# Probabilities copied by pairs of tiles, and a head in another order, in a two-group hybrid attention layer

## The chip, the cores and the metric

The kernel runs on one core of one Trainium2 chip. The metric is the device time of one execution in microseconds (us); lower is better. The times before are those of three runs.

## The reference, cut to what matters

One encoder layer is applied to two groups of 1024 rows (`prompt` and `sample`, called group 0 and group 1 here) with the same weights; the model width is 1024.

```python
mod = silu(c) @ w_ada + b_ada
shift, scale, gate = split(mod, 3)
h = rms_norm(x, norm_g) * (1 + scale) + shift
qa, ka, va, za, qb, kb, vb, zb, ga, gb = split(h @ w_in)
# branch A: 8 query heads, 2 key heads of 64; RMS norm of q and k, axial rotary positions
oa = gqa_attention(qa, ka, va) * silu(za)
# branch B: 4 heads, two softmax maps each, p0 - lam * p1, values of 128
ob = diff_attention(qb, kb, vb, lam)
ob = rms_norm(ob, subln_g) * (1 - lam_init) * silu(zb)
merged = sigmoid(ga) * (oa @ w_proj_a) + sigmoid(gb) * (ob @ w_proj_b)
y = x + gate * (merged @ w_out)
```

Softmax runs over all 1024 keys. Everything is float32; the large projections are done as three products of operands split into a high and a low part.

## The kernel before, in words

**Staging.** Python generators issue small pieces of work, and `weave` interleaves them by a planned count and a lead for each stream (`Z_SHARE`, `ATT_W`, `IN_A` and the other constants at the top are those counts and leads). A scheduler of the language then puts each engine's instructions in order by priority and gives tiles their slots; engines called through `act`, `vec`, `pe` and `dma_next` keep the program's order. All transfers are issued by one queue, SP, in its order.

The stages of a group: the modulation and h (`start`, `start_late` for group 0, `ht_gen` for group 1); the *head* (`head`: keys and values of A, the first queries of A); attention A in 32 units, interleaved with projections (`qa_gen`, `qkb_gen`, `vb_gen`) and with gate-path projections ("z work": `z_gen`, L881, used as filler); attention B in 16 units, of which the last four are interleaved with the rest of the z work and the first merges (`fill`, `gates`, `merge_gen`); then merge and output projection (L1170, L1201) alone.

**Attention.** A *tile* is the softmax of 128 queries over 1024 keys: four matmuls of 512 columns into a two-bank PSUM tile (L908, L909), a maximum on VectorE (L910), an exponential on ScalarE into an SBUF tile p (L912), and in `flip` a 32x32 block transpose on VectorE (L953) and four copies issued by SP (L958) that put the four 32-partition strips where the product with v wants them, in a tile `pT` that holds two tiles (t = 0 and 1). In A a unit is two heads' tiles and the product with v is L984; in B a unit is four tiles (two query tiles, two maps each), the second map is first subtracted (L939, L940, L952), and the product is L1021. The p tiles are 5 buffers of 1024 columns. They also hold the staged first weights (`load_quarters`), the early rows of the head (`row_early`), group 1's x (`ht_gen`) and the sigmoid gates read back in `merge_gen`.

**Group 0's head.** While h of the first 512 rows is made by quarters, `sums_early` already adds up the key/value and first query products of row tiles 0 to 3 (the "early rows"). Then, in `head`: two steps of z, the norm of the late 512 rows (`late[0]`), two steps of z, eight steps of z woven with the late rows' h (`late[1]`), then the early rows' norm and rotary work (`rows`, `rope`, half of it on GpSimd), then the later row tiles woven with z. Each row tile's end, `pairs_T` (L730 to L733), transposes it on TensorE and splits it on ScalarE and VectorE.

**The residual's gate.** `gate_gen` reads the last third of `w_ada` (4 MB) in two halves into weight tiles `wg`, and makes the gate from 32 matmuls of 256 columns (L602) and eight small ones (L611). It is an item of the z work, after the seventh item, and so runs in attention A of group 0.

**The first z weights.** `start` loads them (`load_w`, L244) after the late rows' x (`load_xT0(1)`), splits them on ScalarE (L208) and VectorE (L209), and z begins with them.

Of the kernel before, what the change touches and what calls it, by code (L numbers as in the profile page):

```python
# [20 lines left out]
P = 128  # L21
# [16 lines left out]
    (6, 21, 4, 2, 4, 4),  # L38
    (13, 12, 5, 3, 2, 6),
)  # L40
Z_HEAD = (7, 6)
Z_HEAD_A = (-0.216, -0.32)
ATT_W = (
    (0.893, 1.067, 1.068, 1.192, 1.03, 1.769),
    (1.237, 1.862, 1.041, 1.418, 0.645, 1.256),
)
IN_A = (
    (0.205, -0.07, 0.861, 0.05, 0.25, 0.15),
    (0.125, -0.05, 0.368, 0.3, -0.03, 0.694),
)  # L50
Z_A = (
    (0.2, 0.05, 0.62, -0.05, -0.1, -0.05),
    (-0.215, 0.07, 0.2, 0.16, -0.3, -0.1),
)
LAST_ATT = (46, 40)
LAST_FILL = (20, 25)
GATED_A = (0.063, -0.144)
LATE_A = 1.197
QUARTER_P = 202
KV_STEPS = 12  # L60
GATE_AT = 6
FIRST_ATT = 12
FIRST_A = 0.26
TAIL = (3, 3)
TAIL_A = (0.92, 1.2)
LAG = 2
Z_FIRST = (12, 6)
Z_FIRST_A = (0.017, -0.452)
# [44 lines left out]
def kernel(ctx: ExitStack, tc: tile.TileContext, t: dict):  # L113
# [7 lines left out]
    ppool = ent(tc.tile_pool(name="ppool", bufs=5))  # L121
# [42 lines left out]

    def ptile():
        return ppool.tile([P, 1024], F32, tag="p", name=nm("p"))
# [4 lines left out]
    def halves(pt):  # L171
        return pt[:, :1024], pt[:, 1024:]

# [45 lines left out]
    def load_quarters(mat, col):  # L219
# [3 lines left out]
        sts = [x.rearrange("p (c n) -> p c n", c=2) for _ in range(2) for x in halves2(ptile())]  # L223
# [7 lines left out]
    def load_w(pieces, room=None):  # L231

        if room is None:
# [5 lines left out]
        for q in range(4):  # L239
# [7 lines left out]
            split_w(w, q, st)  # L247
        return [w[c // 2][:, c % 2] for c in range(NCH)]
# [191 lines left out]
    def start(ht):  # L440
# [63 lines left out]
        kva_w.append((load_w(w_cols(w_in, (z_col(Z_ORDER[0]), 256)), room=(utile(), utile())),))  # L504
        sq = late_squares(xT[1])
        return lambda: inv_rms(sq, pe), lambda rs: start_late(ht, xT[1], rs)
# [80 lines left out]
    def gate_gen():  # L587
        for half in range(2):
            w = wpool.tile([P, NCH, 512], F32, tag="w", name=nm("wg"))
            for q in range(4):  # L590
                row, col = q * 256, 2 * D + half * 512
                dma(
                    w[:, q * 2 : q * 2 + 2],
                    w_ada[row : row + 256, col : col + 512].rearrange("(c p) n -> p c n", p=P),
                )
            for n in (half * 2, half * 2 + 1):
                cols = slice(n % 2 * 256, n % 2 * 256 + 256)
                acc = gbank()[:, :256]
                nc.vector.memset(acc, 0.0)
                for q in range(2):  # L600
                    for c in range(4):
                        nc.tensor.matmul(  # L602
                            acc[32 * c : 32 * c + 2], cT[:, q * 4 + c], w[:, q * 4 + c, cols], start=(q == 0),
                            stop=(q == 1), tile_position=(0, 32 * c),
                        )
                    yield 1
                part = rtile()[:, :256]
                nc.vector.tensor_copy(part, acc)
                ps = gbank()[:, :4].rearrange("p (c g) -> p c g", g=2)
                for c in range(2):  # L610
                    nc.tensor.matmul(ps[:, c, :], part[:, c * P : (c + 1) * P], two, start=True, stop=True)  # L611
                cs = slice(n * 2, n * 2 + 2)
                nc.vector.tensor_tensor(
                    out=gatec[:, cs], in0=ps, in1=bcol[:, 2, cs].unsqueeze(2).to_broadcast([P, 2, 2]), op=ALU.add
                )
                nc.vector.tensor_scalar(out=gatec[:, cs], in0=gatec[:, cs], scalar1=0.5, scalar2=None, op0=ALU.mult)
# [812 lines left out]
```

## Time and profile before

| what | value |
|---|---|
| median of three runs | 1884.54 us (1883.9 to 1887.2) |
| the profiled execution's own time | 1887.84 us |
| its span | 1885.6 us |
| TensorE busy | 1852.3 us, 98% of the span |
| VectorE / ScalarE / GpSimd busy | 65% / 45% / 19% |
| copies of p to pT | 768, of 128 KB |

The profile is of one execution. PE is TensorE, PEld its weight loads, DVE VectorE, ACT ScalarE, POOL GpSimd, SPq the queue that issues transfers. In a timeline row the first two columns are start and length in us, then engine, line, operation, output<-input, shape, a count where like instructions follow each other, and in brackets the idle time before them and what ended it. A busy TensorE is not one at its peak: its clock can be halved, which the column PEclk of a windows view shows.

### The profile page before, as it was taken

What the parts mean: (1) busy time and instruction counts of PE and PEld (TensorE: products, weight loads), DVE (VectorE), ACT (ScalarE), POOL (GpSimd) and SP (SyncE); (2) the same over time, 40 slices, a digit from 0 to 9 for tenths busy, and PEclk for the clock granted to TensorE, in tenths of its full rate; (3) what the DMA queues carried; (4) which work ended last, traced back from release to release, by engine and by line L of the source; (5) the groups of instructions that cost most, each with busy time, mean ns of one, the idle gap of its engine ahead of it and who ended that gap; (6) DMA issues with size and microseconds to landing.
All of it is one profiled execution on the core that took longest, in us unless ns stands there. A gap on an engine that the chain in (4) does not pass through costs nothing.

```text
span 1885.6 us, 32132 instructions
## 1 busy us (share of the span) xinstructions
PE 1852.3 (98%) x11516; PEld 1599.4 (85%) x11516; DVE 1228.1 (65%) x1904; ACT 843.1 (45%) x1801; POOL 364.2 (19%) x692
## 2 busy tenths in 40 slices
PE   9999999999999999999999999999999999999999
PEld 7888888877889998788889888888888989877887
DVE  4756776465478677877464777666547767786731
ACT  3544554443456555524223555444445545552210
POOL 0342200011335152100134210000233513210000
PEclk9999999999999999999999999999999999999999
DMA  9225676676254536887531467776524344579532
GB/s 333 83 72 138 162 201 180 173 215 166 71 134 105 130 91 182 254 286 236 190 122 51 127 180 197 196 181 179 158 78 121 98 107 115 156 230 302 168 106 78
DMA packets 277612, 299.54 MB, mean 159 GB/s; under 512 B 37648, under 2 KB 228304, under 8 KB 277456
## 3 DMA queue, kind: packets, MB, share of 16 engines
q1 hardware_dynamic: 277456, 297.51, 55.6%
q8 instruction: 92, 1.51, 0.3%
q14 instruction: 64, 0.52, 0.1%
HBM read 137.91 MB, written 42.04 MB: 95 GB/s over the span
## 4 chain that ended last, share of the span: by engine, by line
PE 76%; DMA 7%; DVE 7%; SPq 3%; issue 3%; POOL 2%; ACT 2%; DVEq 0%; ACTq 0%; POOLq 0%
PE f L881 21%; PE f L670 18%; PE f L1201 6%; PE a L984 6%; PE f L1170 5%; PE s L908 5%; PE s L909 5%; PE a L1021 4%; PE s L1201 3%; DMA row<-zd 2%; PE s L1170 2%; DVE m L910 2%; SPq L958 1%; SPq L109 1%; DMA st<-in_w_in_dram 1%
## 5 line engine op out<-in xcount | busy, mean ns | idle before, releaser
L881 PE MATMUL f<-u,w 128*128 128x512 f32 x2088 | 524.9, 394 | 0.3 <-DVE u L733 0.3
L670 PE MATMUL f<-w,u 128*128 128x256 f32 x3264 | 448.2, 285 | 0.3 <-ACT ev L863 0.3
L881 PEld LDWEIGHTS f<-u,w 128*128 128x128 f32 x2088 | 382.7, 188 | 76.0 <-PE f L730 0.7
L670 PEld LDWEIGHTS f<-w,u 128*128 128x128 f32 x3264 | 425.2, 191 | 18.4 <-issue 1.4
L910 DVE TENSOR_REDUCE m<-s 128x1 f32<-128x1024 f32 x256 | 309.7, 1218 | 112.6 <-PE s L909 110.6
L953 DVE STREAM_TRANSPOSE p<-p 128x1024 f32<-128x1024 f32 x192 | 238.5, 1242 | 45.8 <-ACT p L912 42.1
L909 PE MATMUL s<-u,sw 128*128 128x512 f32 x512 | 202.9, 398 | 0.0
L209 DVE TENSOR_TENSOR w<-st,w 128x512 fp32r<-128x512 f32 x184 | 123.3, 699 | 82.4 <-ACT w L208 81.8
L208 ACT ACTIVATE w<-st 128x512 fp32r<-128x512 f32 x184 | 107.6, 626 | 133.5 <-DMA st<-in_w_in_dram 60.6
L912 ACT ACTIVATE p<-s,m,rsA 128x1024 f32<-128x1024 f32 x128 | 154.4, 1206 | 5.7 <-DMA q<-p 2.2
L912 ACT ACTIVATE p<-s,m,rsB 128x1024 f32<-128x1024 f32 x128 | 154.4, 1206 | 4.0 <-DMA q<-p 0.5
L695 POOL TENSOR_TENSOR rsB<-ss,nhalf 128x4 f32<-128x4 f32 x64 | 66.4, 1038 | 457.0 <-DVE ss L694 442.7
L1170 PE MATMUL f<-u,w 128*128 128x512 f32 x588 | 142.4, 391 | 0.2 <-DVE u L1181 0.2
L1021 PE MATMUL a<-q,u 128*128 128x256 f32 x512 | 126.1, 388 | 7.5 <-DMA q<-p 4.1
L1170 PEld LDWEIGHTS f<-u,w 128*128 128x128 f32 x588 | 109.9, 188 | 23.6 <-DVE u L1181 0.6
L984 PE MATMUL a<-q,u 128*64 128x128 f32 x2048 | 121.8, 276 | 4.0 <-DMA q<-p 3.9
L984 PEld LDWEIGHTS a<-q,u 128*64 128x64 f32 x2048 | 113.2, 138 | 14.6 <-issue 13.3
L733 DVE TENSOR_TENSOR u<-f,u 64x256 fp32r<-64x256 f32 (+1 forms) x208 | 83.7, 407 | 62.8 <-ACT u L732 57.5
L1021 PEld LDWEIGHTS a<-q,u 128*128 128x128 f32 x512 | 96.6, 194 | 23.0 <-issue 5.3
L1201 PE MATMUL f<-u,w 128*128 128x512 f32 x480 | 111.2, 389 | 0.0
L909 PEld LDWEIGHTS s<-u,sw 128*128 128x128 f32 x512 | 96.6, 189 | 16.2
L908 PE MATMUL s<-u 128*128 128x512 f32 x256 | 107.2, 421 | 2.6 <-ACT p L912 2.5
(208 smaller groups left out, 2152.1 us busy)
## 6 DMA issues: line engine op xcount, KB each, us to landing
q<-p SPq DMA_DIRECT2D x768, 128.0 KB, 2.8
st<-in_w_in_dram SPq DMA_DIRECT2D x128, 256.0 KB, 3.2
zd<-ev SPq DMA_DIRECT2D x96, 256.0 KB, 2.3
sw<-u SPq DMA_DIRECT2D x256, 64.0 KB, 2.1
p<-zd SPq DMA_DIRECT2D x64, 256.0 KB, 5.1
u<-in_w_ada_dram SPq DMA_DIRECT2D x16, 512.0 KB, 8.8
od<-oo SPq DMA_DIRECT2D x64, 128.0 KB, 2.6
st<-in_w_in_dram SPq DMA_DIRECT2D x64, 128.0 KB, 2.9
```

What stands on the lines that cost most here:

```text
L209: nc.vector.tensor_tensor(out=wl, in0=st, in1=wh.bitcast(F32), op=ALU.subtract)
L670: nc.tensor.matmul(ps, lt[c][:, sl], w[c][:, wi, :], start=(k == 0), stop=(k == 23))
L881: nc.tensor.matmul(ps, w[c][:, wi, e * P : (e + 1) * P], rt[c], start=(k == 0), stop=(k == 23),)
L908: nc.tensor.matmul(s[:, sl], q, k[:, sl], start=True, stop=False)
L909: nc.tensor.matmul(s[:, sl], sw, k[:, sl], start=False, stop=True)
L910: nc.vector.tensor_reduce(out=m, in_=s, axis=AX.X, op=ALU.max, negate=True)
L912: nc.scalar.activation(pt.rearrange("p (j c a) -> p j c a", j=4, c=8), s.rearrange("p (c a j) -> p j c a", c=8, j=4), AF.Exp, scale=rs, bi ...
L953: nc.vector.transpose(pt, pt)
L984: nc.tensor.matmul(acc[e * 64 : e * 64 + 64, n * P : n * P + P], u["v"](k), blocks[n][:, e, k], start=(k == 0 and n == 1), stop=(k == 7 an ...
L1021: nc.tensor.matmul(acc, u["v"][:, k], pT[:, k], start=(k == 0), stop=(k == 7))
L1170: nc.tensor.matmul(ps, w[:, c, wi, d * P : (d + 1) * P], o[:, oi, :], start=(k == 0), stop=(k == 11))
L1201: nc.tensor.matmul(ps, w[c][:, wi, e * P : (e + 1) * P], m[:, mi, :], start=(k == 0), stop=(k == 23))
```

## The change

- p tiles become two buffers of 2048 columns that hold a pair (t = 0 and 1), and one buffer of 1024 columns (`p1pool`) for the second map in B. The exponential writes its tile in four blocks of 256 columns, 512 apart, so that one copy per 32-partition strip moves both tiles: four issues of 256 KB per pair, after the second transpose, in place of four of 128 KB after each.
- `gate_gen` moves into group 0's head: weights in two halves of 2 MB into tiles of `upool`, issued in program order, the matmuls in the way of `ada_half` (8 of 512 columns for each half), the copy on ScalarE. The `wg` tiles go.
- The early rows' norm and rotary work becomes a stream `early_rows` of eight steps, woven with the late rows' h, the eight z steps and the gate's first half; the gate's second half is woven with the later row tiles.
- The first z weights: three of four quarters are issued ahead of the late rows' x.
- `merge_gen` reads four gates at a time, for the first branch into a tile of `upool` and for the second into a pair tile.
- The counts and leads are others: z steps in group 0 after the first twelve are 14+6 in the head (12+6 before), then 3 x (4, 17, 5, 1, 6) by phase (3 x (6, 21, 4, 2, 4) before, where 8 steps were the gate's).

```diff
-    (6, 21, 4, 2, 4, 4),
+    (4, 17, 5, 1, 6, 4),
...
-LAST_ATT = (46, 40)
-LAST_FILL = (20, 25)
+LAST_ATT = (47, 41)
+LAST_FILL = (23, 28)
...
-LATE_A = 1.197
+LATE_A = 1.334
+EARLY_A = 0.939
...
-GATE_AT = 6
+GATE_A = (0.074, -0.836)
...
-Z_FIRST = (12, 6)
-Z_FIRST_A = (0.017, -0.452)
+Z_FIRST = (14, 6)
+Z_FIRST_A = (-0.245, -0.338)
...
-    ppool = ent(tc.tile_pool(name="ppool", bufs=5))
+    ppool = ent(tc.tile_pool(name="ppool", bufs=2))
+    p1pool = ent(tc.tile_pool(name="p1pool", bufs=1))
...
+    def p2tile():
+        return ppool.tile([P, 2048], F32, tag="p", name=nm("p"))
     def ptile():
-        return ppool.tile([P, 1024], F32, tag="p", name=nm("p"))
+        return p1pool.tile([P, 1024], F32, tag="p1", name=nm("p1"))
...
-        for q in range(4):
+        def load(q):
             st = spool.tile([P, 2, 256], F32, tag="st", name=nm("st"))
...
+        if room:
+            for q in range(3):
+                load(q)
+            yield
+        for q in range(4):
+            if q == len(sts):
+                load(q)
+            split_w(w, q, sts[q])
...
             q_load(q)
+        z_first = load_w_steps(w_cols(w_in, (z_col(Z_ORDER[0]), 256)), room=(utile(), utile()))
+        next(z_first)
         xT.append(load_xT0(1))
...
+    def gate_gen(cpad):
         for half in range(2):
...
+                wt = chunks4(utile().bitcast(F32))
+                wts.append(wt)
+                for c in (0, 2):
+                    row = q * 512 + c * P
+                    dma_next(wt[:, c : c + 2], w_ada[row : row + 256, col : col + 512].rearrange("(c p) n -> p c n", p=P))
+            yield 1
+            acc = ada_half(wts[1], cpad, 1, ada_half(wts[0], cpad, 0))
+            yield 1
+            part = rtile()
+            nc.scalar.activation(part, acc, AF.Copy)
+            yield 1
+            ps = gbank()[:, :8].rearrange("p (c g) -> p c g", g=2)
+            for c in range(4):
+                nc.tensor.matmul(ps[:, c], part[:, c * P : (c + 1) * P], two, start=True, stop=True)
...
-            pt.rearrange("p (j c a) -> p j c a", j=4, c=8), s.rearrange("p (c a j) -> p j c a", c=8, j=4),
+            pt.rearrange("p j (c a) -> p j c a", c=8), s.rearrange("p (c a j) -> p j c a", c=8, j=4),
...
-        pt = ptile()
+        if i == 0:
+            u["p"] = p2tile()
+        both = u["p"].rearrange("p (j t f) -> p t j f", j=4, t=2)
...
+        pt = ptile().rearrange("p (j f) -> p j f", j=4) if m else both[:, t]
...
         nc.vector.transpose(pt, pt)
-        if t == 0:
+        if t:
             u["pT"] = pair(F32R)
-        dst = u["pT"].bitcast(F32).rearrange("p (i t f) -> p i t f", i=4, t=2)
-        for i in range(4):
-            dma(dst[:, i, t], pt[i * 32 : i * 32 + 32])
+            for i in range(4):
+                dma(u["pT"].bitcast(F32)[:, i * 512 : i * 512 + 512], u["p"][i * 32 : i * 32 + 32])
...
+                    if d == 0:
+                        gg = chunks4(p2tile() if br else utile().bitcast(F32))
+                        for a in range(4):
+                            dma(gg[:, a, :], st["gbd" if br else "gad"][(dt_ + a, hf)])
...
+        def early_rows(*gens):
+            for gen in gens:
+                for _ in range(4):
+                    held[0] = True
+                    drain(islice(gen, 3))
+                    held[0] = False
+                    yield 1
...
+            gate = late[2]
+            next(gate)
             drain(islice(zs, 2))
-            weave((islice(zs, 12 - 2 - 2), 12 - 2 - 2, 0.0), (late[1](rs), 4, LATE_A))
-            held[0] = True
-            drain(islice(kva, 12), islice(qa, 12))
-            held[0] = False
-            weave((kva, 15, 0.0), (islice(zs, Z_FIRST[0]), Z_FIRST[0], Z_FIRST_A[0]))
+            weave((islice(zs, 12 - 2 - 2), 12 - 2 - 2, 0.0), (late[1](rs), 4, LATE_A), (early_rows(kva, qa), 8, EARLY_A), (islice(gate, 3), 3, GATE_A[0]))
+            next(gate)
+            weave((kva, 15, 0.0), (islice(zs, Z_FIRST[0]), Z_FIRST[0], Z_FIRST_A[0]), (islice(gate, 3), 3, GATE_A[1]))
             next(qa)
...
-            items.insert(GATE_AT + 1, gate_gen())
```

More of the change, by code (lines that the diff above doesn't have):

```diff
@@ L172, in halves, with fours @@
         return pt[:, :1024], pt[:, 1024:]
+    def fours(pt):
+        return [pt[:, i * 512 : i * 512 + 512] for i in range(4)]
     def halves2(pt):
@@ L222, in load_quarters @@
         w = [w[:, q * 2 : q * 2 + 2] for q in range(4)]
-        sts = [x.rearrange("p (c n) -> p c n", c=2) for _ in range(2) for x in halves2(ptile())]
+        sts = [x.rearrange("p (c n) -> p c n", c=2) for x in fours(p2tile())]
         def load(q):
@@ L231, in load_w, with drain_last, load_w_steps @@
     def load_w(pieces, room=None):
+        return drain_last(load_w_steps(pieces, room))
+    def drain_last(steps):
+        for w in steps:
+            pass
+        return w
+    def load_w_steps(pieces, room=None):
         if room is None:
@@ L246, in load_w @@
             assert off == 256
-            split_w(w, q, st)
-        return [w[c // 2][:, c % 2] for c in range(NCH)]
+            sts.append(st)
+        if room:
[6 more added lines that the diff above has]
+            split_w(w, q, sts[q])
+        yield [w[c // 2][:, c % 2] for c in range(NCH)]
     def w_cols(mat, *cols):
@@ L584, in load_tables_A @@
             st[name] = tab
-    def gate_gen():
+    def gate_gen(cpad):
         for half in range(2):
[L589 to L616, printed above, removed]
@@ new lines, in gate_gen @@
+            col = 2 * D + half * 512
+            wts = []
+            for q in range(2):
+                wt = chunks4(utile().bitcast(F32))
[7 more added lines that the diff above has]
+            part = rtile()
@@ L620, in ht_gen @@
         for tt in range(NTT):
-            xt = ptile()
+            if tt % 2 == 0:
+                xts = halves(p2tile())
+            xt = xts[tt % 2]
             dma(xt, x_sample[tt * P : (tt + 1) * P])
@@ L639, in ht_gen @@
         for c in range(NCH):
-            xt = ptile()
+            if c % 2 == 0:
+                xts = halves(p2tile())
+            xt = xts[c % 2]
             dma(xt, xT_in[g][c * P : (c + 1) * P])
@@ L681, in row_early @@
         if not spare:
[L682 removed]
+            spare.extend(fours(p2tile()))
         return spare.pop(0)
```

38 lines of the change are left out of this document (21 added, 17 removed).

## The prediction

> **What bounds the kernel now.** I read the page's first two parts, then TensorE's waits, then its timeline wherever it stood idle, and last, for each of these places, the queue or engine that came late.
>
> ```profile
> span 1885.6 us, 32132 instructions
> PE 1852.3 (98%) x11516; PEld 1599.4 (85%) x11516; DVE 1228.1 (65%) x1904; ACT 843.1 (45%) x1801; POOL 364.2 (19%) x692
> ```
>
> TensorE is the bound: of the span it stands idle 1885.6 - 1852.3 = 33.3 us. Nothing that shortens another engine's work counts unless one of these idle stretches hangs on it. What ends them:
>
> ```profile
> PE a L1021 <- DMA q<-p: 4.1, 3, 2.7
> PE a L984 <- DMA q<-p: 3.9, 2, 2.3
> PE s L908 <- ACT p L912: 3.8, 4, 1.6
> PE a L1021 <- DVE r L939: 2.9, 1, 2.9
> PE f L602 <- DMA wg<-in_w_ada_dram: 1.4, 3, 0.7
> ```
>
> Columns are the total, the number of times and the longest. The copies of p end 8.0 us of idle time, but five times only, out of 64 products with v. The places, in order of time:
>
> ```profile
> 48.33 1.05 PE L109 MATMUL f<-two,row 128*128 128x2 f32 x8 [1.73 <-ACT row L109]
> 50.76 5.86 PE L881 MATMUL f<-u,u 128*128 128x512 f32 x18
> 64.41 5.73 PE L881 MATMUL f<-u,u 128*128 128x512 f32 x24
> 90.84 0.43 PE L730 MATMUL f<-ident,p 128*128 128x128 f32 x2 [0.89 <-POOL p L784]
> 119.69 0.33 PE L730 MATMUL f<-ident,row 128*128 128x128 f32 x1 [2.34 <-DVE u L733]
> 266.37 0.50 PE L908 MATMUL s<-u,u 128*128 128x512 f32 x1 [0.83 <-ACT p L912]
> 299.98 5.38 PE L984 MATMUL a<-q,u 128*64 128x128 f32 x64 [2.35 <-DMA q<-p]
> 420.62 3.91 PE L984 MATMUL a<-q,u 128*64 128x128 f32 x64 [1.51 <-DMA q<-p]
> 781.12 5.38 PE L1021 MATMUL a<-q,u 128*128 128x256 f32 x16 [2.65 <-DMA q<-p]
> 823.28 3.69 PE L1021 MATMUL a<-q,u 128*128 128x256 f32 x16 [0.77 <-DMA q<-p]
> 1692.19 0.50 PE L908 MATMUL s<-u 128*128 128x512 f32 x1 [1.63 <-ACT p L912]
> 1701.81 5.38 PE L1021 MATMUL a<-q,u 128*128 128x256 f32 x16 [2.88 <-DVE r L939]
> ```
>
> A stall costs more than its idle time. The same 16 matmuls of L1021 took 5.38 us after 2.65 us idle and 3.69 us after 0.77: 1.69 more. The windows view shows why:
>
> ```profile
> 51.00:54.60 3.60, 3.60 (x10) 2.79 (x10) 3.36 (x8) 3.60 (x8) 0.00 (x0) 0.56 0.51 153
> 122.80:126.30 3.50, 3.50 (x19) 3.40 (x19) 1.64 (x4) 1.12 (x3) 0.00 (x0) 0.56 0.51 100
> 300.00:305.40 5.40, 5.40 (x65) 5.23 (x66) 0.35 (x1) 0.56 (x2) 0.00 (x0) 0.69 0.72 209
> 1075.00:1400.00 325.00, 325.00 (x2454) 282.27 (x2453) 203.84 (x263) 155.03 (x325) 33.66 (x63) 1.00 0.63 166
> ```
>
> The third number from the end is the granted clock: 0.56 and 0.69 in the few us behind the stalls of 1.73, 2.34 and 2.35 us, which is 3.2 to 3.4 us at half speed (3.6 x 0.44 / 0.5 and 5.4 x 0.31 / 0.5). So a stall of some 2 us costs its length plus 1.7. The last row is group 1's attention A, with the same copies: TensorE busy 325 of 325 us. There the pairs can win nothing; all of the gain has to come from the places above.
>
> **The change part by part.** The sum is made against the profiled execution's 1887.84 us (its span and 2.2 us around it), 3.3 above the median of the runs.
>
> *First z weights ahead of the late rows' x: -3.5.* ScalarE runs in order:
>
> ```profile
> 47.16 0.63 ACT L208 ACTIVATE u<-st 128x512 fp32r<-128x512 f32 x1 [6.86 <-DMA st<-in_w_in_dram]
> 47.70 0.58 ACT L109 ACTIVATE row<-f 128x512 f32<-128x512 f32 x1
> 37.99 9.15 DMA st<-in_w_in_dram
> ```
>
> The copy `row`, which ends the modulation's last quarter, stands behind the split of z's first weights, and these, issued at 37.99 behind 2 MB of x, land at 47.14. TensorE waits 1.73 us for `row`, and the 18 matmuls behind ran at half clock: 5.86 us, where 24 later took 5.73, that is 18 x 0.239 = 4.3 (1.6 more, 1.7 by the clock). With the weights ahead of x the wait has no cause. What is late next: x, by the 768 KB moved ahead of it; it is read by ScalarE's squares after the last quarter, with the z matmuls of the early rows as cover. Ends: -1.7 (the clock window falls elsewhere) and -3.5.
>
> *The gate moved: -3.7.*
>
> ```profile
> L602 PE MATMUL f<-wg,cT 128*2 128x256 f32 x64 | 6.0, 378 | 1.4 <-DMA wg<-in_w_ada_dram 1.4
> 43.06 1.92 PE L109 MATMUL f<-u,at 128*32 128x512 f32 x16
> ```
>
> The 32 matmuls of 256 columns (64 records) cost 6.0 us. The second row is 8 matmuls of 512 columns by `ada_half` (16 records); the gate now takes 16 of them, twice that: 3.8. That is -2.2; the eight small sums stay. The 1.4 us of waiting for `wg` goes, with most of what the eight 512 KB loads do to SP and to weight tiles there: -1.5. In the head the two halves are filler: each half's loads are four issues more on SP, behind the z weights of the second item and ahead of nothing that TensorE waits for in the trace. ScalarE gets two copies and VectorE loses some, all under z matmuls. If that cover is gone, TensorE waits for 2 MB at the head's start. Ends: -5 and 0.
>
> *Early rows beside the late rows' h: -3.5.* Now their rotary work starts late on GpSimd and TensorE runs out of z at its end:
>
> ```profile
> 80.22 0.70 POOL L695 TENSOR_TENSOR rs<-ss,nhalf 128x2 f32<-128x2 f32 x1 [13.72 <-ACT u L109]
> 119.05 0.59 POOL L719 TENSOR_TENSOR row<-rc,row 128x128 f32<-128x128 f32 x1
> 86.50 0.74 DVE L109 SCALAR_TENSOR_TENSOR u<-u,modc,u 128x512 fp32r<-128x512 f32 x1
> ```
>
> GpSimd is idle 13.7 us before it begins on them; the last key tile is rotated at 119.64, and TensorE, at the end of its 12 z steps, waits 2.34 for it and 1.7 more by the clock; another 0.89 at 90.84. Starting 10 us earlier and two more z steps (each 8 matmuls of 0.239: 1.9) cover 3.8 us, more than the 2.34. That would be -0.9 - 2.3 - 1.7 = -4.9. Against it, VectorE makes the last piece of late h at 87.2, which the later row tiles need, and the early rows' share of VectorE now lies beside it. Ends: -4.9 and +6 (a rival below). I take -3.5, nearer the first, because the scheduler already put part of these rows ahead of 86.50.
>
> *Half the copies, in attention A of group 0: -5.*
>
> ```profile
> L958 SPq DMA_DIRECT2D q<-p x768: 542/602/1864, 135.3 to 1721.7; - x192
> L953 DVE STREAM_TRANSPOSE p<-p x192: 1217/1245/1248, 134.0 to 1716.1; 128x1024 f32<-128x1024 f32 x192
> 286.56 2.58 SPq L958 DMA_DIRECT2D q<-p  x4
> 289.83 7.68 SPq L958 DMA_DIRECT2D q<-p  x12
> q<-p SPq DMA_DIRECT2D x768, 128.0 KB, 2.8
> sw<-u SPq DMA_DIRECT2D x256, 64.0 KB, 2.1
> ```
>
> An issue takes SP 602 ns. I take the same for one of twice the bytes, since the number of rows written (128) stays, so 384 fewer are 231 us of SP; were it twice as long, SP would win nothing. The stall at 299.98 is SP's: it had fallen behind, issued sixteen copies of four tiles to 297.5, and the product waited for the last to land. As pairs, eight issues, it is through 4.8 us sooner, more than the 2.35. So 2.35 + 1.7 go; of the 0.83 at 266.37 and the 1.51 at 420.62 (both behind the same queue) I count half: 1.2. Sum -5.2, taken as -5. Cost: the copies are 256 KB. From 64 to 128 KB the landing grew 0.7 us (2.1 to 2.8), so another 128 KB costs between 0 and 1.4; I take 0.7, the middle. Tile t = 0 can no longer go ahead, but the products use both tiles. Behind the waiting SP stand only loads for later items.
>
> Two pair buffers in place of five tiles: a unit's first exponential now waits for the pair two units before. Group 1's 32 units of A lie about in the 325 us window above, some 10 us apart; transpose, four issues and landing after a unit's last exponential are 1.25 + 2.4 + 3.5 = 7.2, so under 3 us are left, and I count nothing. If that cover is gone, each us of it stops ScalarE once a unit. Writing in four blocks costs nothing while ScalarE (45%) and VectorE (65%) hide it; 10% on a transpose would be 0.12 us a tile.
>
> *The last units of B: -2.* Both groups: 2.65 + 0.77 there are copies, 1.63 and 2.88 are VectorE's and ScalarE's order, 1.7 twice the clock: 11.3 in all. The queue is lighter, the four gates no longer take p tiles, and group 0 keeps two more z steps for it (144 steps less 12, 20 and 99 leave 13; 152 with the gate's less 12, 18 and 111 left 11), 3.8 us of cover. But the landing is later and VectorE's order is drawn anew. Ends -11 and +25 (the third rival); I take -2, near nothing, because the copies that a product waited for were the last of its pair before as well.
>
> *New stalls: +3.* Another order brings its own. I charge one of the size of the smallest above, 0.8, with a clock window, rounded up.
>
> Sum: -3.5 - 3.7 - 3.5 - 5 - 2 + 3 = -14.7. 1887.84 - 14.7 = 1873.1; less the 3.3 of the profiled execution, 1870.
>
> **The rivals.**
>
> *The copies were hidden anyway.* Group 1's attention A has no stall with all 768 issues in place, which speaks for it; the sixteen issues at 286.56 speak against. Then only the first z weights and the matmuls of the gate stay, and new stalls take 3: -3.5 - 2.2 + 3 = -2.7, or 1882.
>
> *The head gets slower.* VectorE and GpSimd hinder each other:
>
> ```profile
> 66.53 0.29 DVE L784 TENSOR_TENSOR p<-p,rs 128x128 f32<-128x128 f32 x1
> 94.74 0.54 DVE L784 TENSOR_TENSOR row<-row,rs 128x128 f32<-128x128 f32 x1 [1.93 <-POOL rs L695]
> 94.67 0.46 POOL L709 TENSOR_TENSOR rc<-p,tab 128x128 f32<-128x128 f32 x1
> ```
>
> The same VectorE product took 0.29 alone and 0.54 beside GpSimd. Late h is 16 operations of 0.74; if a dozen lose 0.25 each that is 3 us, and 3 us of the early rows' own VectorE work slips ahead: late h ends 6 us later, with TensorE waiting. Then +6 stands for -3.5: 1870 + 9.5 = 1879.5. The Trainium skill, SBUF — State Buffer, section "SBUF: two separate sides", says the two engines take a shared pair of ports as an exclusive lock, so that the loser blocks for the whole instruction; by that rule this rival would be the full price. The 0.54 agrees with it.
>
> *Landing decides, slower than before.* The last four units of B in each group have the least z to cover a late pT. If the copies of all eight units land 1.4 us later than now, with a clock window for each, that is 8 x 3.1 = 25; with the first z weights, the gate and attention A kept (-12) it gives +13, 1897. It overtakes the gains once four of the eight stall so. Against it: the last copy of a pair is also the last now, and SP is freer. The Trainium skill, same page, "Door 1: The DMA port swizzle", says 32 partitions reach only 8 of 16 ports, some 218 GB/s; an estimate from that page is 0.6 us more for 128 KB more. No row here shows 256 KB from 32 partitions.
>
> **How the numbers follow.** Forecast as summed 0.53, copies hidden 0.17, head slower 0.15, landing 0.15. The likeliest gives 1870, itself good for 1862 to 1878. The range runs to 1886, which takes in the second and the first rival and leaves most of the third out, and down to 1860 for larger gains in the last units. A measurement tells 0.2% here, 3.8 us: faster means under 1880.8. Faster: 0.53 + 0.15 + 0.06 of the hidden case = 0.74; same 0.11 + 0.03 = 0.14; slower 0.12.
>
> **What would show it.** TensorE idle under 24 us in place of 33.3; no wait for `row` before 50 us and the clock at 1.00 there; no matmul on `wg`; no wait before the key tiles' last transposes near 119; 384 copies of 256 KB at about 600 ns of SP and some 3.5 us to landing; no 5.38 us train of L984. It is wrong if the exponentials wait for the copies (ScalarE's waits grow from a few us to tens), if late h ends after 95 us with TensorE idle, or if the products in the last units wait for copies more than 4 us in all.

## The result and the profile after

The changed kernel takes 1989.95 us, median of five runs, against 1884.54 before: 1.0559 times as long, interval 1.0538 to 1.0581. It lost 105 us where 15 were to be won. Its profiled execution has a span of 1992.1 us. The page's first part and its chain:

```profile
span 1992.1 us, 31283 instructions
PE 1881.6 (94%) x11484; PEld 1618.3 (81%) x11484; DVE 1226.8 (62%) x1892; ACT 843.9 (42%) x1803; POOL 366.7 (18%) x692
...
PE 55%; DMA 18%; SPq 11%; DVE 9%; issue 3%; ACT 3%; POOL 1%; DVEq 0%; ACTq 0%; POOLq 0%
PE f L700 13%; PE f L911 10%; DMA q<-p 9%; PE a L1017 6%; PE f L1235 5%; SPq L991 5%; PE f L1204 4%; PE s L1235 4%; PE a L1054 3%; SPq L794 3%; PE s L938 3%; DVE m L940 3%; PE s L939 3%; DMA st<-in_w_in_dram 2%; DMA row<-zd 2%
```

TensorE stands idle 1992.1 - 1881.6 = 110.5 us, 77.2 more than before, and is busy 29.3 us longer with 32 fewer matmuls. The sum is the 106.5 us of span. Most of the longer busy time is the half clock: the mean granted clock fell from 0.995 to 0.984, and 0.016 x 1992.1 less 0.005 x 1885.6 is an estimated 22 us. TensorE is no longer the bound everywhere: DMA and SP hold 29% of the chain, 10% before. Of the waits, those around the copies of p:

```profile
ACT p L942 <- DMA q<-p: 79.3, 33, 4.4
PE a L1017 <- DMA q<-p: 54.5, 25, 4.5
PE a L1054 <- DMA q<-p: 25.6, 16, 2.9
PE s L938 <- ACT p L942: 9.3, 9, 2.0
```

L1017 is the product with v in attention A (L984 before), L1054 that in B (L1021), L942 the exponentials. The products wait 80.1 us for the copies of p where they waited 8.0, and the exponentials 79.3 us where they waited 2.7. The page's DMA part (KB of one issue, median us from issue to landing), and the copies in the tile's view (ns of an issue on SP: least, median, most):

```profile
q<-p SPq DMA_DIRECT2D x384, 256.0 KB, 4.8
zd<-ev SPq DMA_DIRECT2D x96, 256.0 KB, 3.4
od<-oo SPq DMA_DIRECT2D x64, 128.0 KB, 4.1
sw<-u SPq DMA_DIRECT2D x256, 64.0 KB, 2.1
```

```profile
L991 SPq DMA_DIRECT2D q<-p x384: 543/650/2250, 151.5 to 1827.0; - x192
```

Twice the bytes land after 4.8 us, not 2.8. SP's issue has a median of 650 ns but goes up to 2250: it is held up. How four issues lie in a row, and what follows from it, the timeline and the chain of waits in attention A of group 0 show:

```profile
303.76 4.24 SPq L991 DMA_DIRECT2D q<-p  x4
308.05 0.59 SPq L1024 DMA_DIRECT2D od<-oo  x1
308.69 4.10 SPq L794 DMA_DIRECT2D sw<-u  x4
312.88 4.28 SPq L991 DMA_DIRECT2D q<-p  x4
```

```profile
309.50 2.00 SPq L794
...
312.88 0.59 SPq L991
...
315.45 4.88 DMA q<-p
320.33 0.24 issue
320.58 5.38 PE a L1017 x64
```

Four issues of a pair take SP 4.2 us (the median of all 96 pairs too), not 2.4. The swap copies behind them (L794: they bring q with its halves exchanged) are held too, one of 64 KB took 2.00 us to issue, so the next pair's copies start at 312.88, and the one issued at 315.45 lands 4.88 us later. TensorE waits 2.65 us for it and runs its train, the 64 matmuls of one product, at half clock:

```profile
301.73 3.71 PE L1017 MATMUL a<-q,u 128*64 128x128 f32 x64 [2.39 <-DMA q<-p]
...
320.58 5.38 PE L1017 MATMUL a<-q,u 128*64 128x128 f32 x64 [2.65 <-DMA q<-p]
```

The train before it kept its clock after 2.39 us of idle time. Of the 14 whole trains of L1017 behind 2.15 to 3.95 us of idle time, eight took 5.26 to 5.38 us and six 3.71; the length of the stall does not tell which. This loop goes round for most of attention A, whose products wait 25 times. In group 1, where TensorE was busy 325 of 325 us before:

```profile
1150.00:1350.00 200.00, 177.19 (x1297) 150.80 (x1298) 119.12 (x132) 84.25 (x174) 7.63 (x11) 0.98 0.66 164
```

The head did more or less what it should. Its timeline:

```profile
44.03 0.74 PE L110 MATMUL s<-w,u 128*128 128x256 f32 x4 [1.20 <-DVE u L110]
...
48.08 0.95 PE L110 MATMUL f<-two,row 128*128 128x2 f32 x8
...
86.58 0.62 PE L700 MATMUL f<-w,u 128*128 128x256 f32 x3 [0.70 <-DVE u L110]
...
124.31 1.86 PE L911 MATMUL f<-u,w 128*128 128x512 f32 x7 [0.65 <-DVE u L763]
```

The wait of 1.73 us for `row` and that of 2.34 near 119 are gone. But new, shorter ones (1.20 at 44.03, four of 0.4 to 0.7 from 85 to 89) take nearly all of it back: TensorE's waits in the first 135 us sum to 7.6 us where they were 8.2. The clock won nothing either: it is now halved behind the waits near 88 and 132 us, where the granted clock reads 0.50 and 0.51 (88.7 to 92.1 and 133.0 to 136.4 us).

### The profile page after: what moved, and what is told of

Read it like the earlier page. It is cut to its first block, busy times and chain, and to the rows that moved or that the text cites. A ratio compares the mean times of both kernels' runs of the same rounds, so it can differ in the third digit from the quotient of the medians.

```text
span 1992.1 us, 31283 instructions
## 1 busy us (share of the span) xinstructions
PE 1881.6 (94%) x11484; PEld 1618.3 (81%) x11484; DVE 1226.8 (62%) x1892; ACT 843.9 (42%) x1803; POOL 366.7 (18%) x692
## 4 chain that ended last, share of the span: by engine, by line
PE 55%; DMA 18%; SPq 11%; DVE 9%; issue 3%; ACT 3%; POOL 1%; DVEq 0%; ACTq 0%; POOLq 0%
PE f L700 13%; PE f L911 10%; DMA q<-p 9%; PE a L1017 6%; PE f L1235 5%; SPq L991 5%; PE f L1204 4%; PE s L1235 4%; PE a L1054 3%; SPq L794 3%; PE s L938 3%; DVE m L940 3%; PE s L939 3%; DMA st<-in_w_in_dram 2%; DMA row<-zd 2%
## 5 line engine op out<-in xcount | busy, mean ns | idle before, releaser
L911 PE MATMUL f<-u,w 128*128 128x512 f32 x2016 | 511.8, 396 | 1.9 <-DVE ev L895 1.3
L911 PEld LDWEIGHTS f<-u,w 128*128 128x128 f32 x2016 | 372.1, 189 | 76.5 <-DVE ev L895 1.9
L942 ACT ACTIVATE p<-s,m,rsA 128x1024 f32<-128x1024 f32 x128 | 154.3, 1206 | 91.7 <-DMA q<-p 79.3
L1017 PE MATMUL a<-q,u 128*64 128x128 f32 x2048 | 136.0, 295 | 56.5 <-DMA q<-p 54.5
L1017 PEld LDWEIGHTS a<-q,u 128*64 128x64 f32 x2048 | 126.8, 150 | 68.3 <-issue 57.2
L1054 PE MATMUL a<-q,u 128*128 128x256 f32 x512 | 132.9, 399 | 27.2 <-DMA q<-p 25.6
L942 ACT ACTIVATE p<-s,m,rsB 128x1024 f32<-128x1024 f32 x128 | 154.3, 1205 | 4.6 <-DVE p L986 1.0
L1204 PE MATMUL f<-u,w 128*128 128x512 f32 x588 | 143.1, 393 | 2.0 <-DVE u L1215 2.0
L1054 PEld LDWEIGHTS a<-q,u 128*128 128x128 f32 x512 | 98.7, 199 | 47.9 <-issue 30.5
L1204 PEld LDWEIGHTS f<-u,w 128*128 128x128 f32 x588 | 109.7, 188 | 26.6 <-DVE u L1215 2.8
L720 ACT ACTIVATE row<-f 128x256 f32<-128x256 f32 (+1 forms) x104 | 38.5, 370 | 162.7 <-PE f L700 161.5
```

The lines of the kernel that those rows point to most:

```text
L911: nc.tensor.matmul(ps, w[c][:, wi, e * P : (e + 1) * P], rt[c], start=(k == 0), stop=(k == 23),)
L942: nc.scalar.activation(pt.rearrange("p j (c a) -> p j c a", c=8), s.rearrange("p (c a j) -> p j c a", c=8, j=4), AF.Exp, scale=rs, bias=m, ...
L1017: nc.tensor.matmul(acc[e * 64 : e * 64 + 64, n * P : n * P + P], u["v"](k), blocks[n][:, e, k], start=(k == 0 and n == 1), stop=(k == 7 an ...
L1054: nc.tensor.matmul(acc, u["v"][:, k], pT[:, k], start=(k == 0), stop=(k == 7))
L1204: nc.tensor.matmul(ps, w[:, c, wi, d * P : (d + 1) * P], o[:, oi, :], start=(k == 0), stop=(k == 11))
```

## The experiments

**Which part lost the time.** My theory after the result: the pairs. The rival: the order that the new counts draw. First the changed kernel with single p tiles and copies of 128 KB again, and the gates read two at a time again, as they share the p tiles, all else as changed; then before with nothing but the pairs.

```diff
 copies_back (from after)
-    ppool = ent(tc.tile_pool(name="ppool", bufs=2))
+    ppool = ent(tc.tile_pool(name="ppool", bufs=5))
...
-        if t:
+        if t == 0:
...
+        for i in range(4):
+            dma(dst[:, i, t], pt[i * 32 : i * 32 + 32])
 pairs_only (from before): these lines the other way round
```

> The changed kernel with five p tiles of 1024 columns and four 128 KB copies per tile again, as before; head, gate, first z weights and counts stay as changed. If the pairs are the loss (copies or buffers), TensorE's waits for copies of p fall from 80 us to under 10 and the time to 1870-1885. If the new head or the new counts are the loss, it stays near 1990.

> The kernel before with pair tiles, two pair buffers and four 256 KB copies per pair only. If the pairs are the loss: 1970-2000, with TensorE's waits for copies near 80 us. If the loss needs the changed head or counts: 1880-1900.

copies_back: 1898.2 us, ratio 1.0084 [1.0062, 1.0106]. pairs_only: 2010.3, 1.0675 [1.0647, 1.0702], with 76.0 us of the products' waits for the copies. The pairs alone cost more than the whole change.

**The rest of the change.** copies_back is still 13.6 us slower than before. head_g0 gives group 1 its old counts and leads; the other three take one part of the head each, alone, to the kernel before (gate_only with 3 x 18 z steps in the second phase for 3 x 21, since 8 of those were the gate's).

```diff
 head_g0 (from copies_back)
-    (1.237, 1.927, 1.041, 1.418, 0.645, 1.256),
+    (1.237, 1.862, 1.041, 1.418, 0.645, 1.256),
-LAST_FILL = (23, 28)
+LAST_FILL = (23, 25)
...
 zfirst_only (from before)
+        z_first = load_w_steps(...); next(z_first)   # ahead of load_xT0(1)
 early_only (from before)
-            drain(islice(kva, 12), islice(qa, 12))
+            weave(..., (early_rows(kva, qa), 8, 0.939))
 gate_only (from before)
-            items.insert(GATE_AT + 1, gate_gen())
+            weave(..., (islice(gate, 3), 3, GATE_A[0]))
```

> The kernel with single-tile copies and the changed head, with group 1's counts and leads as in the kernel before. If the 13 us that were left come from group 1's new order, it falls to 1886 to 1890; if they come from the new head and group 0's counts, it stays at 1895 to 1900.

> The kernel before with the first z weights issued ahead of the late rows' x, nothing else. By the prediction -3.5: 1880 to 1882. If the wait only moves to another operation: 1883 to 1886.

> The kernel before with the early rows woven beside the late rows' h, nothing else (counts as before). By the prediction -3.5 (-4.9 to +6). If VectorE and GpSimd hinder each other and late h ends later: 1886 to 1890.

> The kernel before with the gate moved into the head in the new form, and 18 in place of 21 for group 0's second phase, whose eight gate steps are gone. By the prediction -3.7 (-5 to 0). If the head has no place for its loads and matmuls: 1885 to 1890.

head_g0: 1887.6, 1.0027 [1.0014, 1.0039]. So 10.6 of the 13.6 us are group 1's counts, which stand for another kernel's copies, and the new head with group 0's counts costs 3. Each part alone on the old counts is slower: zfirst_only 1894.1, 1.0052 [1.0040, 1.0065]; early_only 1902.3, 1.0092 [1.0076, 1.0107]; gate_only 1925.5, 1.0221 [1.0207, 1.0235]. Waits of gate_only, then of early_only:

```profile
PE s L904 <- ACT p L908: 16.6, 12, 2.8
PE f L726 <- POOL row L715: 5.5, 5, 2.4
```

```profile
PE f L730 <- POOL row L719: 6.4, 4, 4.5
```

Not all of these waits are at the edited place: each edit draws the order of later stages anew. gate_only's attention A of group 0 runs 339 us from the start of the first exponential to that of the last, 322 before. How much of each loss is the part itself and how much the new order is not shown.

**What of the pair costs.** A pair differs in four ways: two pair buffers, all copies behind the second transpose, 256 KB to an issue, and rows of 2 KB written instead of 1. Theory first: the later landing, with too few buffers. pairs_each keeps the pair buffers but copies each tile after its own transpose; strip_order only reads the 32-partition strips in the order 0, 2, 1, 3; before_order does so in the kernel before; late_small and small_stripwise split each copy of the pair in two.

```diff
 strip_order (from after), before_order (from before)
-            for i in range(4):
+            for i in (0, 2, 1, 3):
 pairs_each (from after)
-        if t:
+        if t == 0:
...
+            dma(dst[:, i, t], pt[i * 32 : i * 32 + 32])
 late_small (from after)
+            for h in range(2):
+                for i in range(4):
+                    dma(dst[:, i, h], u[h][0][i * 32 : i * 32 + 32])
 small_stripwise: the two loops exchanged
```

> The changed kernel, pair tiles and two pair buffers kept, but each tile copied after its own transpose with four copies of 128 KB. Buffer theory (two pairs hold too few tiles, the exponentials wait): it stays at 1960-1990. Copy theory (256 KB out of 32 partitions lands late, 4.8 us, and only after the second transpose): landing back to 2.8 us and time 1870-1900.

> The changed kernel with the four strips of a pair copied in the order 0, 2, 1, 3, so that neighbours in the queue read from different halves of the partitions. If a shared read path of partitions 0 to 63 and of 64 to 127 makes the 256 KB copies slow, landing falls from 4.8 to under 4 us and the time by 20 us or more. If the rate is set elsewhere, or the buffers bind, no change: 1980-1995.

> The kernel before with strips in the order 0, 2, 1, 3. Copies of 128 KB are held back by the issues (0.6 us each), so their landing of 2.8 us falls by 0.3 at most; 1880 to 1886. If the read side limits here too: 1870 to 1880.

> The changed kernel with a pair copied after the second transpose, but as eight copies of 128 KB. If what costs is that the first tile no longer goes ahead, it stays near 1990 or gets slower (SP 4.9 us per pair behind the second transpose); if the size of the copies costs, it comes near the 1907 of copies tile by tile.

> The changed kernel with each strip of a pair copied in two issues of 128 KB, one behind the other: strips 0,0,1,1,2,2,3,3, in place of four issues of 256 KB in the order 0,1,2,3. The source partitions are read in the same order for the same bytes; only the size of one issue is halved. The version with eight issues in the order 0,1,2,3,0,1,2,3 took 1903.7 us. Theory 'size': what costs is the issue of 256 KB itself (SP held at the issue, the next transfers behind it): 1900 to 1915 us, landing near 2.8 us, SP's median issue near 0.61 us. Rival 'order': what costs is that all bytes of one strip of 32 partitions go before the next strip's, so that few of the ports work at a time: 1970 to 1995 us with landings above 3.5 us. In between (1930 to 1960) both count, as the 1948.6 us of the strips in the order 0,2,1,3 suggest.

pairs_each: 1906.7, 1.0123 [1.0104, 1.0142]. late_small: 1903.7, 1.0117 [1.0089, 1.0145]. small_stripwise: 1904.4, 1.0112 [1.0093, 1.0130]. strip_order: 1948.6, 1.0343 [1.0319, 1.0368]. before_order: 1881.9, 0.9990 [0.9977, 1.0004], no difference. late_small, its DMA part and waits:

```profile
q<-p SPq DMA_DIRECT2D x768, 128.0 KB, 2.8
od<-oo SPq DMA_DIRECT2D x64, 128.0 KB, 2.6
```

```profile
ACT p L942 <- DMA q<-p: 32.5, 14, 4.4
PE a L1019 <- DMA q<-p: 3.3, 3, 1.8
```

The buffers are not the main loss: with them the exponentials still wait 32.5 us for copies, but TensorE's products in attention A wait 3.3, and the kernel takes 5.5 us more than copies_back. small_stripwise, at the same time as late_small, speaks against the order in which one strip's bytes go, though not fully: in at least 24 of the 64 pairs of its attention A two or more copies were issued before the second transpose ended. Those were the first tile's, so SP did not go strip by strip there. strip_order's products still wait 47.6 us in all, where the changed kernel's wait 80.1:

```profile
PE a L1017 <- DMA q<-p: 28.7, 20, 3.4
PE a L1054 <- DMA q<-p: 18.9, 13, 2.9
```

late_small and small_stripwise left one confusion. In their programs, the four copies of a pair's first tile wait for that tile's transpose alone, so they may go ahead of the second; in the changed kernel none can. small_both takes that head start away: a VectorE instruction that reads the second tile writes one column of the first back unchanged. big_1kb keeps four issues of 256 KB but writes rows of 1 KB (the two tiles apart in the transposed buffer); small_2kb has eight issues of 128 KB with rows of 2 KB, out of 16 partitions each.

```diff
 small_both (from late_small)
+            x0, x1 = u[0][0][:, 0, :1], pt[:, 0, :1]
+            nc.vector.scalar_tensor_tensor(out=x0, in0=x1, scalar=0.0, in1=x0, op0=ALU.mult, op1=ALU.add)
 big_1kb (from after)
+            dst = u["pT"].bitcast(F32).rearrange("p (t i f) -> p i t f", i=4, t=2)
...
+                dma(dst[:, i], u["p"][i * 32 : i * 32 + 32])
 small_2kb (from after)
+                for h in range(2):
+                    dma(u["pT"][h * 64 : h * 64 + 64, i * 512 : i * 512 + 512], u["p"][i * 32 + h * 16 : i * 32 + h * 16 + 16])
```

> late_small (eight issues of 128 KB per pair in the order of the tiles, 1903.7 us) with one more VectorE instruction per pair: it reads a column of the second tile and writes a column of the first back unchanged, so that all eight copies wait for both tiles' transposes. In late_small, as its program lists its waits, the first four copies waited for the first tile's transpose alone, and SP issued them ahead of the second. Theory 'head start': what the pairs of 256 KB lose is that no copy goes ahead of the second transpose, so that 1 MB (7.3 us alone) and not 512 KB (4.5 to 5 us) is left behind it: 1950 to 1995 us, with the exponentials' waits for copies over 55 us. Rival 'size': the issue of 256 KB itself is what costs: 1900 to 1912 us. Between, 1920 to 1945: both.

> The changed kernel with its four issues of 256 KB per pair, but written in rows of 1 KB (two per partition and strip: the two tiles lie apart in the pair's transposed buffer) in place of rows of 2 KB. Theory 'issue size': an issue of 256 KB holds SP and the engines whatever its rows: 1980 to 1995 us, or slower by the doubled rows, SP's median issue over 0.61 us, landing 4.5 us or more. Rival 'rows': the rows of 2 KB are what costs: 1900 to 1920 us.

> The changed kernel with eight issues of 128 KB per pair, each out of 16 partitions, written in rows of 2 KB to half of the partitions. Theory 'issue size': 1900 to 1930 us (the 16 partitions alone cost 1 us per MB by themselves: 8.3 against 7.3 us), landing 3.1 us. Rival 'rows': 1980 us or more, with SP held at its issues as with the four.

small_both: 1894.6, 1.0063 [1.0044, 1.0082]. big_1kb: 2023.0, 1.0753 [1.0732, 1.0774]. small_2kb: 1947.2, 1.0340 [1.0325, 1.0356]. small_both's waits, then big_1kb's (its products in A and in B), its DMA part and its issues on SP:

```profile
ACT p L942 <- DMA q<-p: 38.1, 13, 9.5
PE a L1021 <- DMA q<-p: 3.8, 2, 2.1
```

```profile
PE a L1018 <- DMA q<-p: 68.3, 27, 4.9
PE a L1055 <- DMA q<-p: 33.6, 18, 3.4
```

```profile
q<-p SPq DMA_DIRECT2D x384, 256.0 KB, 5.0
```

```profile
L992 SPq DMA_DIRECT2D q<-p x384: 609/989/2301, 148.8 to 1855.2; - x192
```

The wide rows are not the cause: with 256 KB to an issue and narrow rows it is worse still. Five versions with issues of 256 KB take 1949 to 2023 us; four with the same pair buffers and 128 KB out of 32 partitions take 1895 to 1907. small_2kb falls between: its 16-partition copies are slower by themselves (below).

This looks like the size of the issue, but the edits change more: in each of those four the trace lists TensorE's matmuls in another order than in the changed kernel. In the changed kernel, strip_order and big_1kb, on the other hand, the traces list the same instructions in the same order on every engine; only the copies differ, so these three show what a later landing costs. The table follows the 32 products of attention A from the end of their last exponential, as medians of the timelines: when the last copy landed (where the trace has its landing, 14 to 23 of the 32), and for how long TensorE had other work before the product.

| run | order of instructions | last landing | other work | products wait, A and B | time |
|---|---|---|---|---|---|
| before | its own | 8.45 us | 9.9 us | 8.0 us | 1884.5 us |
| strip_order | the changed kernel's | 10.11 | 9.5 | 47.6 | 1948.6 |
| changed kernel | the changed kernel's | 11.02 | 9.5 | 80.1 | 1990.0 |
| big_1kb | the changed kernel's | 11.46 | 9.5 | 101.9 | 2023.0 |
| late_small | its own | 8.74 | 10.3 | 4.6 | 1903.7 |
| small_both | its own | 11.24 | 12.5 | 4.9 | 1894.6 |

In one order, landing 0.9 us later costs 41 us (strip_order against the changed kernel) and 0.4 us more another 33 (big_1kb). late_small escapes because its copies land sooner, with 0.8 us more of other work. small_both's land as late as the changed kernel's; its products do not wait because 3 us more of other work stand ahead of them. So small_both does not price the head start, of which late_small made some use (29 of its 64 pairs in A have a copy issued before the second transpose ended), and it does not show that the size of an issue costs.

**What the size of an issue does to the copies.** sw_on_act issues the swap copies from ScalarE's queue, out of SP's way. copies_alone2 and copies_stream compute nothing of the layer; they time copies alone: the first in groups of 1 MB with a VectorE instruction that waits for each, the second as a stream through two buffers. An earlier form of the first, copies_alone, had transfers of x beside its first two groups, but also two groups of one copy at a time, which are used below.

```diff
 sw_on_act (from after)
-                dma(sw[a, m].bitcast(F32), q[b, sl].bitcast(F32))
+                nc.scalar.dma_start(sw[a, m].bitcast(F32), q[b, sl].bitcast(F32))
 copies_alone2, copies_stream (of new): a pair as in after
+    for i in (0, 1, 2, 3):
+        dma(d[:, i * 512 : i * 512 + 512], src[i * 32 : i * 32 + 32])
```

> The changed kernel with the copies that swap the halves of q (64 KB, four for each pair of tiles) issued by ScalarE in place of SP; the pairs' copies stay at four issues of 256 KB. Theory 'queue on SP': the swap copies stand on SP behind the held-up issues (4.1 us for four), and SP is held by them in turn; away from SP about 2.5 us less stand in the loop once a pair: 1940 to 1970 us, and the exponentials' waits for copies fall under 60 us (79.3 now). Rival 'engines': the transfers themselves queue on the DMA engines, whoever issues them: 1980 to 1995 us, and the swap copies land later than 2.1 us. Rival 'ScalarE': four issues of some 0.6 us stop ScalarE's exponentials: slower than 1995 us.

> Only SBUF to SBUF copies again (x is copied to y at the end), now with all transfers in program order, since transfers of x ran beside groups da and db in the first of these runs. da: four strips of 256 KB in the order 0, 1, 2, 3; db: order 0, 2, 1, 3; dc: strip 0 four times; dd: 256 KB from all 128 partitions, four times; de, df: as da, db in eight copies of 128 KB; dg, dh: as da, de with a 64 KB copy (ea, eb) behind; di: eight copies of 128 KB in rows of 2 KB from 16 partitions each; dj: strips 0 and 1 only, dk: strips 0 and 2 only. Read-side theory: da about as dc (7.6 us from first issue to last landing), db 5 to 6.5, dk shorter than dj by 0.5 to 1, and ea lands 2 us later than eb. If the halves do not matter: da = db = dc.

> Copies by themselves, nothing of the layer is computed: pairs of 1 MB follow each other through two buffers without a stop, ten times each: pa four issues of 256 KB, pb eight of 128 KB; pc and pd the same with a weight load of 256 KB from DRAM behind each pair; pe and pf with four swap copies of 64 KB and the load behind each pair. A pair alone took 7.3 us in both forms. Theory 'mixed traffic': four and eight issues are equal alone, but with loads and swap copies between them the four large ones hold the others up: pa and pb within 0.2 us per pair, pe at least 0.8 us longer than pf, la and sa landing 1 us or more later than lb and sb. Rival 'no difference in a stream': pe and pf within 0.3 us, so that the loss in the kernel comes from what waits for the single transfer and not from the rate. Rival 'large is slower in any stream': pa at least 0.5 us longer than pb.

sw_on_act: 1988.8, 1.0579 [1.0547, 1.0612]: taking the swap copies out of SP's line won nothing. The products wait 47.0 us for pairs, not 80.1, but TensorE is idle 103 us all the same, in another order of its matmuls, and from ScalarE the swap copies land in 3.4 us, not 2.1. copies_alone's single copies (dg 256 KB, dh 128 KB, each out of 32 partitions), then copies_alone2, its DMA part and SP's issues (da four of 256 KB, de eight of 128 KB, dd four of 256 KB from all 128 partitions):

```profile
dg<-src SPq DMA_DIRECT2D x6, 256.0 KB, 3.4
dh<-src SPq DMA_DIRECT2D x6, 128.0 KB, 2.5
```

```profile
da<-src SPq DMA_DIRECT2D x24, 256.0 KB, 4.6
...
dd<-src SPq DMA_DIRECT2D x24, 256.0 KB, 2.5
de<-src SPq DMA_DIRECT2D x48, 128.0 KB, 2.6
...
ea<-src SPq DMA_DIRECT2D x6, 64.0 KB, 3.4
eb<-src SPq DMA_DIRECT2D x6, 64.0 KB, 2.4
```

```profile
L109 SPq DMA_DIRECT2D da<-src x24: 542/914/1637, 3.0 to 53.4; - x24
L109 SPq DMA_DIRECT2D de<-src x48: 542/608/618, 216.5 to 269.1; - x48
```

From first issue to the waiting instruction 1 MB takes 7.25 us in four issues and 7.28 in eight (7.0 in the order 0, 2, 1, 3; 8.3 as small_2kb has it), but 4.45 when each copy reads all partitions. So it is the read out of 32 partitions that limits, and four large issues only move SP's time into the queue: SP is held 0.91 us at the median. A copy of 256 KB alone lands in 3.4 us and behind its like in 4.6: part of the later landing is waiting for the copies ahead. The 64 KB copy behind lands 3.4 us after its own issue behind four (ea) and 2.4 behind eight (eb), but it is also issued sooner: from the first issue of the group it is 7.55 and 7.51 us, the same. The Trainium skill, SBUF — State Buffer, section "Door 1: The DMA port swizzle", gives 32 partitions half of the ports; the 4.6 us against 2.5 of da and dd agree. copies_stream, the first and last of ten waiting instructions each (pe four issues, pf eight, each with four swap copies sa, sb and a weight load):

```profile
224.97 2.29 DVE L109 TENSOR_TENSOR sink<-pe,sink 128x2048 f32<-128x2048 f32 x1 [2.82 <-DMA pe<-src]
...
297.67 2.29 DVE L109 TENSOR_TENSOR sink<-pe,sink 128x2048 f32<-128x2048 f32 x1 [4.18 <-DMA pe<-src]
...
305.84 2.29 DVE L109 TENSOR_TENSOR sink<-pf,sink 128x2048 f32<-128x2048 f32 x1 [4.43 <-DMA sb<-src]
...
382.31 2.29 DVE L109 TENSOR_TENSOR sink<-pf,sink 128x2048 f32<-128x2048 f32 x1 [4.66 <-DMA sb<-src]
```

As a rate the large issues are better: 72.70 / 9 = 8.08 us per pair against 76.47 / 9 = 8.50 (4.82 and 5.25 without swaps and load). So no rate was lost. The single transfer lands later by its own issue (4.6 us against 2.7, the swap copies 2.9 against 2.0), but the pair as a whole does not. Nor is the stream full: one pair with swap copies and one without, each with a load, take 8.08 + 5.43 = 13.5 us in large issues, 8.50 + 5.86 = 14.4 in small ones, of the 18.4 us between two trains of products before (20.3 after, medians of attention A). What attention A waits for is the time from a pair's last exponential to its last landing, not the rate.

**What stays open.** It is shown that the pairs lose the time (copies_back, pairs_only), and that in the changed kernel's order a later landing of the pairs costs it (strip_order, big_1kb). It is not shown that the size of the issue is what makes them late: from first issue to last landing four take 8.05 us in attention A and small_both's eight 7.6. The copies that can no longer go ahead, SP coming to the pair late and the size all go into the 11.0 us, and no run has four issues of 256 KB in the order of small_both, or eight of 128 KB in that of the changed kernel. Why the scheduler put more work ahead of the products for eight issues behind both transposes than for four is not known either.

## Why the prediction was wrong

It said 1870 and the kernel takes 1990. The 105 us split by the runs so: 86.3 four issues of 256 KB in place of eight, with the order of instructions that comes with them (1989.95 - 1903.7), 5.5 the pair buffers and the copies put behind the second transpose (1903.7 - 1898.2), 10.6 group 1's counts, 3.1 the head and group 0's counts. This path takes late_small as the pair with small issues; by small_both the first two are 95.4 and -3.6.

- *Half the copies, -5.* The step that failed is "I take the same for one of twice the bytes, since the number of rows written (128) stays". The row under it gave the issue's time when the queue is free. Four issues took 4.2 us, not 2.4, so SP gained about 1 us on eight, not half: the copies of p take it 387.6 us in all, 478.5 before. The landing grew 2.0 us, not 0.7, outside the bounds of 0 to 1.4. For a copy by itself 0.7 was near (0.9: 2.5 to 3.4 us); what the term left out is the wait behind the other three. So the sum 1.25 + 2.4 + 3.5 = 7.2 us from a unit's last exponential to the landing, which left "under 3 us", measured 11.0 (8.45 before), against 9.5 us of other work for TensorE. It also has nothing for SP being late: the first issue starts 1.4 us after the transpose, in the timeline above behind the swap copies.
- *"There the pairs can win nothing".* True, and only half of the question: a stage where all copies are just hidden (8.45 us under 9.9) has everything to lose. Attention A runs 352.1 and 312.6 us from the start of the first exponential to that of the last in the two groups, 327.7 and 282.8 in late_small: 54 of the 86 us. B has 22.
- *Two pair buffers, counted nothing.* The sign set for this, that ScalarE's waits grow to tens of us, came (79.3). By the runs it is a companion: 32.5 to 38.1 us with the small issues, and little time lost.
- *Landing decides, slower than before: 1897, chance 0.15.* The right mechanism, priced at eight stalls in the last units of B. There were 41 in both attentions.
- *A stall costs its length plus 1.7.* This holds for eight of the 14 trains above, and not for the other six.
- *First z weights, early rows, the gate.* The waits named did go, and the gate's matmuls cost what was said (32 records more by `ada_half`). Of the terms of -3.5, -3.5 and -3.7 nothing is left in head_g0: +3.1 together. New stalls in the head took part of it back (7.6 us of waits against 8.2); where the rest went is not shown.
- *New stalls, +3.* Too small as a term for any edit: on the old counts the parts took 9, 18 and 41 us more than before, and one added VectorE instruction of 0.16 us per pair moved late_small by -9, with the order of TensorE's work.
- *Late h* ended at 87.65, not after 95: the head rival did not come. Its row shows no block for the whole instruction either: VectorE's product ended at 95.28, 0.15 us after GpSimd's at 95.13, and takes 0.29 alone.

## What to carry over

Half as many issues of twice the bytes saved SP little here, since it was held at the larger ones. Before counting issues, work out how long the whole group takes from the instruction that makes the data to the last landing, and set it against the work that the waiting engine has in between. A stage with no stalls at all is where a longer latency costs most, so price the loss there before the gain elsewhere. Where a scheduler draws the order of instructions, two versions that differ in one edit can differ in the order of everything: compare the order in the traces before the time is put down to the edit, and keep some 10 us for any edit.

## What the runs showed of the hardware

- A copy of 256 KB out of 32 partitions lands in 3.4 us alone (128 KB: 2.5) and in 4.6 behind its like, out of 128 partitions in 2.5 behind its like; 1 MB in four such copies takes 7.25 and 4.45 us.
- An issue on SP is not a fixed cost: 0.54 us at the least, 0.91 at the median and up to 1.64 behind large copies, up to 2.25 in the kernel, and it then delays whatever SP issues next.
- With every engine's instructions in the same order, reading the strips in the order 0, 2, 1, 3 took 41 us off the changed kernel (landing 0.9 us sooner in attention A) and nothing off the kernel before (0.9990 [0.9977, 1.0004]).
- Two strips take 4.95 us as 0, 1 and 4.45 as 0, 2.
- As a stream, 1 MB took 4.82 us in four issues and 5.25 in eight; alone it took 7.25 and 7.28.
- Behind 2.15 to 3.95 us of idle time a train of 64 matmuls took 5.26 to 5.38 us eight times and 3.71 six times.
